# Three plain tiles instead of four ahead of the products of halves in four SwiGLU FFNs

## The chip, the cores and the metric

The kernel runs on one core of a Trainium2 chip. The metric is the device time of one execution in microseconds (us). TensorE multiplies, VectorE (DVE in the profile), ScalarE (ACT) and GpSimd (POOL) do elementwise work, SyncE (SP) issues the loads. Each engine works through its own queue in order and waits on semaphores.

## What is computed

A decoder trunk of two layers over 512 tokens and 16 prepended meta tokens, D = 1024, all in float32. Each layer is an FFN, a token mixer (gated linear attention in layer 0, windowed attention over shared keys and values in layer 1) and a second FFN; every part stands between two RMS norms and is added to the residual stream. The four FFNs are what the change is about:

```python
def rmsnorm(x, g):
    y = x * rsqrt(mean(x * x, axis=-1) + EPS)
    return y * g

def swiglu(x, w_in, w_out):              # D = 1024, D_FF = 2816
    gate, up = jnp.split(x @ w_in, 2, axis=-1)
    return (jax.nn.silu(gate) * up) @ w_out

h = h + 0.5 * rmsnorm(swiglu(rmsnorm(h, g[0]), w_ffn_in[layer, 0], w_ffn_out[layer, 0]), g[1])
```

## The kernel before

**Layout.** Tokens run along the free axis, features along the 128 partitions. `H` is the residual stream in eight tiles of 128 features (`KD`), `Y` a block's output. Layer 0 works on two groups of tokens, 272 and 256 (`L0`), layer 1 on 256 and 256 (`L1`) or on 512 at once (`L1W`). `D_FF` is cut into 22 tiles of 128 hidden features (`NFF`).

**Precision.** A float32 product is three matmuls on split operands: `hi` is a rounded copy, `lo` the difference; `hi*hi`, `lo*hi` and `hi*lo` add up in PSUM (`mm3s`, L344). Each split is a copy on ScalarE and a subtraction on VectorE: weights at L236 and L237 (`split_part`) or L255 and L256 (`split_pair`), hidden activations at L446 and L447.

**One FFN** (`ffn`, L754) goes through the hidden tiles in the chunks of `FF_CHUNKS`; after each chunk the hidden tiles so far are multiplied by their rows of `w_out` and added into `Y` (`out_steps`, L658).

- The first chunk, four tiles, is *plain*. `x_first` (L605) does two tiles on the first group of tokens and then on the second, while the block before still finishes; `x_units` (L580) does the two others. The operand `x` here isn't yet scaled by the norm's root: the result is, when it leaves PSUM (L767, L771), so these tiles can start before the root is known. Evacuation is two multiplications by the root, `silu`, a product and a split.
- The later chunks, three times six tiles, use *products of halves* (`class Strassen`, L867). The gate and up matrices of a tile, cut into two halves of D, are a 2 x 2 block matrix; the tokens in two halves make another. The 2 x 2 product takes seven products instead of eight. Each is 12 matmuls of 264 or 256 columns (`product`, L877). Their weights are sums of blocks, formed on VectorE by four additions (`add`, L261) and split into seven parts named 11, s1, s3, s2, 12, s4, 22 (`split_pair`, L246). A tile uses them in the order 11, s1, s2, 12, s3, then 11 of the next tile, s4, 22 (`head`, `body`, `tail`). Between them ScalarE copies bank `a` to `d` (L900) and banks to SBUF (L906, L908), and the products that follow overwrite these banks.

**The right-hand operand.** `right_factors` (L822) makes the operand of the halves while the plain tiles run: it waits for the roots of both groups (`x.rjob`), writes the normalized operand to `xs` with eight operations over all tokens (L847), and then, with differences of blocks (`less`, L843), splits seven operands called 11, t1, 22, t2, 21, t3 and t4 (`part`, L834 and L835). t3 and t4 wait until the plain tiles' matmuls are issued, since they use their space. `ffn` lets all of them be issued before the first product (L797).

**The roots.** At the end of the block before, `Residual.run` (L503) updates `H` group by group, builds the plain operand (`build`, L468 and L469) and sums the squares (L438, L441, L442). `factors` (L479) then makes the root and spreads it to 128 partitions: matmuls give the sums (`st`, L367), eleven or more small operations the root and a diagonal (L375 to L421), a matmul `r` spreads it (L429), and ScalarE copies it to `rt` (L491). `factors` uses GpSimd unless told otherwise; the very first FFN uses VectorE. Between FFN 2 (`l0f1`) or FFN 4 (`l1f1`) and its mixer the second group's root is made on GpSimd, `BEHIND` = 2.2 after the first step of its turn. FFN 3 (`l1f0`) uses the roots that the shared keys and values needed before it.

**What sets the order.** The order of TensorE is written out by the program. `Flow` (L70) keeps an estimated clock that each matmul advances, and side jobs (generators) say by `yield` how long until their next step; `flow.pump` issues what is due between matmuls, `flow.wait` issues jobs until one is finished. The other engines' instructions are ordered by the framework from this. Weights are loaded by SP into `RAWS` = 8 buffers of 512 columns; a split part occupies one of 32 buffers of the pool `hp`, as do z, hidden tiles and scratch. `set_ahead(n, slots)` (L219) limits how many weights are asked for and how many split parts may live at once: 4 in the plain tiles after `x_first`, 8 in the first output projection, `RING` = 10 among the products. `CHAINS` = 2 weight chains are made at once. The last chunk's rows of `w_out` come as `NLAST` units of another layout (`w_last`), read in one packed pass.

Of the kernel before, what the change touches and what calls it, by code (L numbers as in the profile page):

```python
# [13 lines left out]
ALU = mybir.AluOpType  # L14
# [3 lines left out]
D = 1024  # L18
KD = 8
# [1 line left out]
SEQ = 512  # L21
TOK = META + SEQ
NFF = 22
FF_CHUNKS = [(0, 4), (4, 10), (10, 16), (16, 22)]
LAST = 16
NLAST = NFF - LAST
HEADS = 4
RSQRT_MAGIC = float(0x5F3759DF)
# [2 lines left out]
L1W = [(16, 512)]  # L31
SLOTS = 32
RAWS = 8
RING = 10
STEP = 1.1
CHAINS = 2

# [11 lines left out]
NORM = 4.0  # L49
BUSY = 2.6  # L50
SHUT = 5.0
LOW = 1.0
LAG = 5
PERIOD = 3.2
# [79 lines left out]
def trunk_kernel(ctx: ExitStack, tc, a, out, last_out):  # L134
# [32 lines left out]
    def gain(layer, i, k):  # L167
        c = V_GAIN + layer * 48 + i * 8 + k
        return vec[:, c : c + 1]
# [49 lines left out]
    def set_ahead(n, slots=None):  # L219
        ahead[0], limit[0] = n, slots or n  # L220
        room[0].finish(flow)
        room[0] = Job(None)
# [226 lines left out]
    class Operand:  # L449


        def __init__(self, name, gv, groups, rt=None, parts=(1, 2)):
            self.parts = parts
            self.name, self.gv, self.groups, self.tiles = name, gv, groups, [None] * KD
            self.ready = set()
            self.rt = rt

            self.column = None
            self.more = LONGER
            self.rjob = [None] * len(groups)  # L460
            self.accs = [[] for _ in groups]

# [16 lines left out]
        def factors(self, gi, eng=pool):  # L479
            if self.column is not None:  # L480
                o, n = self.groups[gi]
                yield FACT + (ADDED if self.parts[gi] == 1 else 0)
                root(self.accs[gi], n, D, f"{self.name}_{o}", eng, *self.column[gi])
                yield CHAIN
                return
            if self.rt is None:
                self.rt = sm.tile([P, TOK], F32, tag="R", name=f"R_{self.name}", bufs=2)
            o, n = self.groups[gi]
            yield FACT + (ADDED if self.parts[gi] == 1 else 0)
            r = yield from rstd(self.accs[gi], n, D, False, f"{self.name}_{o}", eng, gi * BEHIND if eng is dve else self.more)  # L490
            act.activation(self.rt[:, o : o + n], r[:, :n], AF.Copy)  # L491

        def need(self, gi, k):
# [3 lines left out]
    class Residual:  # L497
# [5 lines left out]
        def run(self, gi, g, sums):  # L503
            o, n = g
            nxt = self.nxt
            if self.turned(gi):
                self.turn(g, sums)
                return
            yield 1.8 + (ADDED if self.parts[gi] == 1 else 0)
            r = yield from rstd(sums, n, D, self.half, f"post_{self.name}{gi}", dve)  # L510
            if nxt is None:
                yield from self.store(gi, g, r)
                return
            for k in range(KD):
                h, y = H[:, k, o : o + n], Y[:, k, o : o + n]
                t = r[:, 256 : 256 + n] if n <= 256 else ps(f"t_{self.name}{gi}{k}")[:, :n]
                dve.tensor_tensor(t, y, r[:, :n], op=ALU.mult)
                dve.tensor_tensor(h, t, h, op=ALU.add)
                nxt.build(gi, k)
                nxt.sumsq(gi, k)  # L520
                yield 1.0
            nxt.rjob[gi] = flow.spawn(nxt.factors(gi), gi * BEHIND)

        def store(self, gi, g, r):
            o, n = g
# [228 lines left out]
    def ffn(x, groups, finish, opening=False, tail=4):  # L754
        set_ahead(8 if opening else 16)

        def evac_to(hids):
            gss = {}

            def evac(i, g, p):  # L760
                o, n = g
                r = x.rt[:, o : o + n]
                if i % 2 == 0:
                    if i not in gss:
                        gss[i] = duo("gu")
                    gs = gss[i][0][:, o : o + n]
                    dve.tensor_tensor(gs, p[:, :n], r, op=ALU.mult)  # L767
                    act.activation(gs, gs, AF.Silu)
                else:
                    gs, us = (t[:, o : o + n] for t in gss[i - 1])  # L770
                    dve.tensor_tensor(us, p[:, :n], r, op=ALU.mult)  # L771
                    dve.tensor_tensor(us, gs, us, op=ALU.mult)
                    split(hids[i // 2], us, g)

            return evac

        jobs = []
        n2 = sum(n for _, n in groups) // 2
        halves = [(groups[0][0], n2), (groups[0][0] + n2, n2)]
        z, plain = {}, Job(None)  # L780

        def new_hid():
            hids.append(pair_tile(f"hid{x.name}_{lo + len(hids)}"))
            return hids[-1]

        for ci, (lo, hi) in enumerate(FF_CHUNKS):
            hids = []
            if ci == 0:
                jobs = x_first(x, 4, evac_to([new_hid() for _ in range(2)]), opening)
                set_ahead(16, 4)  # L790
                factors = flow.spawn(right_factors(x, halves, z, plain))
                for t in range(2, hi):
                    jobs += x_units(x, 2, groups, evac_to([new_hid()]))
                plain.finish(flow)
                set_ahead(16, 8)
            else:
                flow.wait(factors)  # L797
                set_ahead(16, RING)
                tiles = Strassen(z, halves)
                cur = tiles.head(new_hid())  # L800
                while cur:
                    last = len(hids) == hi - lo
                    if last:
                        fin = (finish, KD, True) if lo >= LAST else (None, 0, False)
                        proj = out_steps(hids, groups, x.groups, False, *fin, jobs)
                        end = used[0] + NLAST + tail
                    tiles.body(cur, (lambda: next(proj)) if last else (lambda: None))
                    nxt = None if last else tiles.head(new_hid())
                    jobs.append(tiles.tail(cur, last))
                    cur = nxt  # L810
            if ci == 0:
                out_proj(hids, groups, x.groups, True, jobs=jobs)
                continue
            if lo >= LAST:
                set_ahead(32)
                cap[0] = min(end, len(units))
            for _ in proj:
                pass
# [1 line left out]


    def right_factors(x, halves, z, plain):  # L822
        for job in x.rjob:
            yield job
        (o, n), _ = halves
        xs = [pair_tile(f"xs{x.name}_{k}", F32) for k in range(0, KD, 2)]
        blocks = [[t[:, :, i * n : (i + 1) * n] for t in xs] for i in range(2)]
        b11, b12, b21, b22 = blocks[0][:2], blocks[1][:2], blocks[0][2:], blocks[1][2:]

        def part(name, src, sign=1.0):  # L830
            z[name] = []
            for c, b in enumerate(src):
                w = pair_tile(f"z{x.name}_{name}{c}").rearrange("p a (k t) -> p a k t", k=2)[:, :, :, :n]
                act.activation(w[:, 0], b, AF.Copy, scale=sign)  # L834
                dve.scalar_tensor_tensor(  # L835
                    w[:, 1], b, sign, w[:, 0].bitcast(F32), op0=ALU.mult, op1=ALU.subtract
                )
                z[name].append(w)
                yield STEP

        def less(dst, p, q):
            for d, s, t in zip(dst, p, q):
                dve.tensor_tensor(d, s, t, op=ALU.subtract)  # L843
                yield STEP

        for k in (0, 1, 2, 3, 4, 5, 6, 7):
            dve.scalar_tensor_tensor(  # L847
                xs[k // 2][:, k % 2, : 2 * n], H[:, k, o : o + 2 * n], x.gv(k), x.rt[:, o : o + 2 * n],
                op0=ALU.mult, op1=ALU.mult,
            )  # L850
            yield 0.8
        yield from part("11", b11)
        yield from less(b11, b12, b11)
        yield from part("t1", b11, -1.0)
        yield from part("22", b22)
        yield from less(b12, b22, b12)
        yield from less(b22, b22, b11)
        yield from part("t2", b22, -1.0)
        yield from part("21", b21)
        yield from less(b21, b21, b22)  # L860
        yield plain
        yield from part("t3", b12)
        yield from part("t4", b21, -1.0)
# [618 lines left out]
    ffn(x, L0, fin, True)  # L1482
    x = nxt
    nxt, fin = into("l0f1", 0, 3, False, lambda k: gain(0, 4, k), L0)
    gla(x, fin)
    x = nxt
    nxt, fin = into("kv", 0, 5, True, lambda k: vec[:, V_KVN + k : V_KVN + k + 1], L0, (1, 1))
# [4 lines left out]
    with tc.tile_pool(name="kp", bufs=1) as kp:  # L1492
# [14 lines left out]
        ffn(x, L1W, fin)  # L1507
        x = nxt
        nxt, fin = into("l1f1", 1, 3, False, lambda k: gain(1, 4, k), L1, post=(2, 2))
        flow.wait(placed)  # L1510
        swa(x, kv, fin)
    ffn(nxt, L1W, Residual("out", 1, 5, True))
# [92 lines left out]
```

## Time and profile before

| | us |
|---|---|
| median of 3 runs | 1891.31 (1891.0 to 1892.04) |
| profiled execution, its time | 1890.36 |
| its span, first to last instruction | 1888.6 |
| VectorE busy | 1397.5 |
| ScalarE busy | 1017.7 |

The spans of the FFNs in the profile: the products of halves start at 84.8, 695.5, 1081.8 and 1595.9 us in FFN 1 to 4. How to read it: times in the profile count from the first instruction. PE is TensorE's matmuls, PEld its weight loads beside them. A row of the timeline gives start, length, engine, line, operation, output and inputs by name, shapes and a count, and in brackets the idle time of that engine just before and what ended it. A matmul's length holds the time that its result takes to come out, so the pace of a series is read from its starts. The same holds for VectorE: two operations that don't depend on each other start closer together than their length.

### The profile page before, as it was taken

The page shows a single profiled execution, that of the slowest core. Times are in us where ns is not written, and L with a number is a line of the kernel's source. Part 1 is how long each engine was busy: PE and PEld are TensorE (multiplying, and loading weights), DVE is VectorE, ACT ScalarE, POOL GpSimd, SP SyncE. Part 2 cuts the span into 40 slices and gives each one's busy share as a digit, 9 for nine tenths or more (in the row PEclk, how much of TensorE's full clock was granted, in tenths as well). Part 3 has the DMA queues.
Part 4 walks back from the last instruction along what each step waited for, and adds up shares of the span by engine and source line. Part 5 has one row for each costly group of instructions (what it writes and reads, how often), then busy time and mean ns, then how long its engine had stood idle before and what let it go on. Part 6 is the DMA issues. An engine that isn't in the chain of part 4 may idle for free.

```text
span 1888.6 us, 37662 instructions
## 1 busy us (share of the span) xinstructions
PE 1872.3 (99%) x14645; PEld 1791.3 (95%) x14645; DVE 1397.5 (74%) x2798; ACT 1017.7 (54%) x2273; POOL 196.0 (10%) x398
## 2 busy tenths in 40 slices
PE   8999999999999999999999999999999999999998
PEld 8999999999999999999999898989987898989898
DVE  7885858767564788585887886868766779868685
ACT  5653535653436566353574553535756855636364
POOL 2000000331311300000033000000320140000002
PEclk9999999999999999999999999999999999999999
DMA  4333232422113123233351223333421212333331
GB/s 165 97 98 103 90 107 96 137 68 66 48 59 121 46 90 96 90 101 101 100 175 46 72 86 112 93 110 101 135 74 51 69 46 73 97 106 103 104 113 57
DMA packets 102276, 174.74 MB, mean 93 GB/s; under 512 B 11856, under 2 KB 24016, under 8 KB 102096
## 3 DMA queue, kind: packets, MB, share of 16 engines
q1 hardware_dynamic: 101520, 171.67, 28.4%
q8 instruction: 115, 1.88, 0.4%
q10 hardware_dynamic: 576, 0.65, 0.1%
q14 instruction: 65, 0.53, 0.1%
HBM read 169.66 MB, written 2.10 MB: 91 GB/s over the span
## 4 chain that ended last, share of the span: by engine, by line
PE 87%; DVE 9%; ACT 2%; issue 2%; DMA 0%; POOL 0%; DVEq 0%; SPq 0%; ACTq 0%; POOLq 0%
PE y L172 30%; PE x L172 19%; PE a L172 18%; PE c L172 8%; PE d L172 4%; DVE raw L261 2%; ACT w_s L255 1%; PE o L172 1%; DVE w_s L256 1%; DVE w L256 1%; PE e L172 1%; DVE w L237 1%; PE po L172 1%; PE sa L172 1%; PE ps L172 0%
## 5 line engine op out<-in xcount | busy, mean ns | idle before, releaser
L256 DVE TENSOR_TENSOR w_s<-raw,w_s 128x512 fp32r<-128x512 f32 x288 | 193.8, 690 | 131.3 <-ACT w_s L255 128.9
L172 PE MATMUL y<-hidl0f,w 128*128 128x256 f32 (+1 forms) x2112 | 262.1, 285 | 1.1 <-DVE hidl0f L447 0.9
L172 PEld LDWEIGHTS y<-hidl0f,w 128*128 128x128 f32 x2112 | 259.1, 188 | 2.2 <-DVE hidl0f L447 1.5
L255 ACT ACTIVATE w_s<-raw 128x512 fp32r<-128x512 f32 x288 | 175.2, 628 | 152.3 <-DVE raw L261 139.1
L172 PE MATMUL y<-hidl1f,w 128*128 128x512 f32 (+1 forms) x1344 | 251.3, 346 | 0.3
L237 DVE TENSOR_TENSOR w<-raw,w 128x512 fp32r<-128x512 f32 x376 | 234.9, 654 | 21.9 <-ACT w L236 19.9
L172 PEld LDWEIGHTS y<-hidl1f,w 128*128 128x128 f32 x1344 | 212.7, 188 | 35.0 <-DVE hidl1f L933 1.5
L236 ACT ACTIVATE w<-raw 128x512 fp32r<-128x512 f32 x376 | 206.2, 586 | 39.3 <-PE y L172 29.3
L442 POOL TENSOR_TENSOR acc_post<-acc_post,sq_post 128x256 f32<-128x256 f32 (+1 forms) x77 | 62.9, 817 | 1458.2 <-ACT sq_post L441 1457.4
L261 DVE TENSOR_TENSOR raw<-raw,raw 128x512 f32<-128x512 f32 x288 | 198.0, 687 | 5.5
L256 DVE TENSOR_TENSOR w<-raw,w 128x512 fp32r<-128x512 f32 x216 | 148.4, 687 | 29.8 <-ACT w L255 29.0
L255 ACT ACTIVATE w<-raw 128x512 fp32r<-128x512 f32 x216 | 134.1, 621 | 41.1 <-PE y L172 40.7
L172 PE MATMUL x<-x_l0m,w 128*128 128x272 f32 (+1 forms) x1152 | 152.4, 289 | 0.0
L172 PEld LDWEIGHTS x<-x_l0m,w 128*128 128x128 f32 x1152 | 143.6, 189 | 1.5 <-issue 0.4
L697 DVE TENSOR_TENSOR Y<-y,Y 128x256 f32<-128x256 f32 (+2 forms) x175 | 81.9, 474 | 70.9 <-PE y L172 70.2
L172 PE MATMUL a<-zl0f_t,w_s 128*128 128x264 f32 x864 | 117.2, 285 | 0.0
L172 PE MATMUL a<-zl1f_t,w_s 128*128 128x256 f32 x864 | 114.3, 282 | 0.8 <-ACT c L908 0.5
L172 PEld LDWEIGHTS a<-zl0f_t,w_s 128*128 128x128 f32 x864 | 110.1, 188 | 0.3
L172 PEld LDWEIGHTS a<-zl1f_t,w_s 128*128 128x128 f32 x864 | 107.2, 188 | 2.5 <-ACT c L908 2.2
L172 PE MATMUL x<-x_l0f,w 128*128 128x256 f32 (+1 forms) x768 | 100.6, 291 | 6.2 <-ACT w L236 5.9
L172 PEld LDWEIGHTS x<-x_l0f,w 128*128 128x128 f32 x768 | 97.2, 193 | 7.6 <-ACT w L236 6.2
L172 PE MATMUL x<-x_l1f,w 128*128 128x256 f32 (+1 forms) x576 | 92.9, 321 | 0.0
(511 smaller groups left out, 3257.9 us busy)
## 6 DMA issues: line engine op xcount, KB each, us to landing
raw<-in_w_in SPq DMA_DIRECT2D x352, 256.0 KB, 2.9
raw<-in_w_out SPq DMA_DIRECT2D x96, 256.0 KB, 3.4
raw<-in_w_last SPq DMA_DIRECT2D x48, 256.0 KB, 3.0
raw<-in_gla_in SPq DMA_DIRECT2D x48, 256.0 KB, 3.0
raw<-in_w_out SPq DMA_DIRECT2D x64, 128.0 KB, 2.8
raw<-in_gla_out SPq DMA_DIRECT2D x16, 256.0 KB, 2.9
raw<-in_w_q SPq DMA_DIRECT2D x16, 256.0 KB, 3.8
raw<-in_swa_out SPq DMA_DIRECT2D x16, 256.0 KB, 3.0
```

The lines of the kernel that those rows point to most:

```text
L172: inst = pe.matmul(o, lhs, rhs, start=start, stop=stop, skip_group_check=onto)
L236: act.activation(w[:, 0, :m], raw[:, :m], AF.Copy)
L237: dve.tensor_tensor(w[:, 1, :m], raw[:, :m], w[:, 0, :m].bitcast(F32), op=ALU.subtract)
L255: act.activation(w[:, 0, :512], src, AF.Copy)
L256: dve.tensor_tensor(w[:, 1, :512], src, w[:, 0, :512].bitcast(F32), op=ALU.subtract)
L261: dve.tensor_tensor(dst, dst, src, op=ALU.add)
L442: pool.tensor_tensor(sums[0][:, :n], sums[0][:, :n], t[:, :n], op=ALU.add)
L697: dve.tensor_tensor(y, p[:, :n], y, op=ALU.add)
```

## The change

- `FF_CHUNKS` becomes three plain tiles and then chunks of 6, 6 and 7 tiles of products of halves. So one tile per FFN goes from the plain form to the products; the first output projection covers three tiles (384 columns of `w_out` per unit, not 512), the last one seven (`LAST` = 15, seven `w_last` units).
- `right_factors` writes the normalized operand group by group: after the first group's root eight operations on its tokens, after the second group's root eight on the others, not eight over all after both.
- For the operands of FFN 2 and FFN 4 (`late = dve`) the second group's root is made on VectorE and asked for without the delay `BEHIND`; `SPLIT` = 1.4 is the time allowed before the matmul that spreads it.
- `RING` is 16 less the tiles of the chunk: 10 for six tiles, as before, and 9 for seven.

```diff
-FF_CHUNKS = [(0, 4), (4, 10), (10, 16), (16, 22)]
-LAST = 16
+FF_CHUNKS = [(0, 3), (3, 9), (9, 15), (15, 22)]
+LAST = 15
...
-RING = 10
+RING = 16
...
+SPLIT = 1.4
...
             self.more = LONGER
+            self.late = pool
...
-            r = yield from rstd(self.accs[gi], n, D, False, f"{self.name}_{o}", eng, gi * BEHIND if eng is dve else self.more)
+            r = yield from rstd(self.accs[gi], n, D, False, f"{self.name}_{o}", eng, (SPLIT if self.late is dve else gi * BEHIND) if eng is dve else self.more)
...
-            nxt.rjob[gi] = flow.spawn(nxt.factors(gi), gi * BEHIND)
+            if gi and nxt.late is dve:
+                nxt.rjob[gi] = flow.spawn(nxt.factors(gi, dve))
+            else:
+                nxt.rjob[gi] = flow.spawn(nxt.factors(gi), gi * BEHIND)
...
-                set_ahead(16, RING)
+                set_ahead(16, RING - (hi - lo))
...
     def right_factors(x, halves, z, plain):
-        for job in x.rjob:
-            yield job
...
-        for k in (0, 1, 2, 3, 4, 5, 6, 7):
-            dve.scalar_tensor_tensor(
-                xs[k // 2][:, k % 2, : 2 * n], H[:, k, o : o + 2 * n], x.gv(k), x.rt[:, o : o + 2 * n],
-                op0=ALU.mult, op1=ALU.mult,
-            )
-            yield 0.8
+        for job, (og, ng) in zip(x.rjob, x.groups):
+            yield job
+            for k in range(KD):
+                dve.scalar_tensor_tensor(
+                    xs[k // 2][:, k % 2, og - o : og - o + ng], H[:, k, og : og + ng], x.gv(k), x.rt[:, og : og + ng],
+                    op0=ALU.mult, op1=ALU.mult,
+                )
+                yield 0.4
...
     nxt, fin = into("l0f1", 0, 3, False, lambda k: gain(0, 4, k), L0)
+    nxt.late = dve
...
         nxt, fin = into("l1f1", 1, 3, False, lambda k: gain(1, 4, k), L1, post=(2, 2))
+        nxt.late = dve
```

## The prediction

> **What bounds the kernel now.** I read the busy times and the chain of waits on the page first.
>
> ```profile
> PE 1872.3 (99%) x14645; PEld 1791.3 (95%) x14645; DVE 1397.5 (74%) x2798; ACT 1017.7 (54%) x2273; POOL 196.0 (10%) x398
> PE 87%; DVE 9%; ACT 2%; issue 2%; DMA 0%; POOL 0%; DVEq 0%; SPq 0%; ACTq 0%; POOLq 0%
> ```
>
> TensorE sets the time: less work for it is time won, if it is never kept waiting. DMA and GpSimd are no part of the chain. VectorE's 74% is a mean, so I took the busy time by stage. The first four windows run from the second group's roots (for the third FFN: from the end of its first two tiles) to the first product of halves of FFN 1 to 4; I call such a stretch a head. The fifth is six tiles of products. Columns: stretch, length, then busy time and instruction count of PE, weight loads, DVE, ACT, POOL, the clock, DMA share and GB/s.
>
> ```profile
> 40.55:84.75 44.20, 43.37 (x352) 42.72 (x351) 42.93 (x79) 27.29 (x61) 0.00 (x0) 1.00 0.29 91
> 655.15:695.50 40.35, 40.07 (x328) 39.81 (x327) 38.57 (x73) 25.19 (x57) 0.00 (x0) 1.00 0.24 73
> 1036.90:1081.83 44.93, 44.93 (x199) 36.53 (x198) 40.42 (x69) 24.08 (x46) 0.00 (x0) 1.00 0.21 67
> 1558.71:1595.86 37.15, 37.15 (x163) 30.02 (x161) 35.49 (x61) 22.14 (x42) 0.00 (x0) 1.00 0.22 71
> 84.75:148.20 63.45, 63.45 (x523) 63.45 (x522) 51.28 (x93) 37.41 (x80) 0.00 (x0) 1.00 0.33 105
> ```
>
> In the heads VectorE is busy 42.93 of 44.20, 38.57 of 40.35, 40.42 of 44.93 and 35.49 of 37.15 us; among the products only 51.28 of 63.45. So the heads are full on both engines, and the change shortens exactly these. DMA moves at a share of 0.33 at most, so loads are no limit.
>
> **What TensorE saves.** Timeline rows: start, length, line, tile, shape, count.
>
> ```profile
> 654.35 17.12 PE L172 MATMUL x<-x_l0f,w 128*128 128x272 f32 x138
> 675.79 19.75 PE L172 MATMUL y<-hidl0f,w 128*128 128x256 f32 x160 [0.28 <-DVE hidl0f L447]
> 695.50 1.62 PE L172 MATMUL a<-zl0f,w 128*128 128x264 f32 x12
> 696.97 1.63 PE L172 MATMUL c<-zl0f_t,w_s 128*128 128x264 f32 x12
> 1557.90 15.66 PE L172 MATMUL x<-x_l1f,w 128*128 128x512 f32 x66
> 1573.40 22.50 PE L172 MATMUL y<-hidl1f,w 128*128 128x512 f32 x96
> 1595.86 1.57 PE L172 MATMUL a<-zl1f,w 128*128 128x256 f32 x12
> 1597.27 1.59 PE L172 MATMUL c<-zl1f_t,w_s 128*128 128x256 f32 x12
> ```
>
> Layer 0: a plain tile is 96 matmuls, 272 and 256 columns in turn, at 17.12/138 = 0.123 us: 11.8 us. As products it is seven runs of 12 matmuls that start 1.47 us apart (695.50, 696.97): 10.3 us. Saved: 1.5 us. Layer 1: 48 matmuls of 512 columns; 66 of them take 1557.90 to 1573.40, 0.235 us each: 11.3 us; seven runs 1.41 us apart are 9.9 us. Saved: 1.4 us. The output projection has the same matmuls, only in other chunks. Four FFNs: 2 x 1.5 + 2 x 1.4 = **5.8 us** saved.
>
> [...]
>
> **What the shorter head costs.** The products begin earlier by the whole fourth plain tile and by its share of the first output projection: in layer 0 by 11.8 + 48 x 19.75/160 = 17.7 us, in layer 1 by 11.3 + 24 x 22.50/96 = 16.9 us. By then VectorE must have made the operands z. Its own relief, with the price of an operation taken as the distance of two starts:
>
> ```profile
> 1561.63 0.42 DVE L767 TENSOR_TENSOR gu<-x,R_l1f 128x256 f32<-128x256 f32 x1
> 1561.97 0.41 DVE L771 TENSOR_TENSOR gu<-x,R_l1f 128x256 f32<-128x256 f32 x1
> 1576.85 3.69 DVE L237 TENSOR_TENSOR w<-raw,w 128x512 fp32r<-128x512 f32 x6
> 40.55:84.75 44.20, 7.88 (x12) 1.00 0.29 91
> 655.15:695.50 40.35, 5.14 (x8) 1.00 0.24 73
> 1036.90:1081.83 44.93, 4.98 (x8) 1.00 0.21 67
> 1558.71:1595.86 37.15, 4.97 (x8) 1.00 0.22 71
> ```
>
> 256 columns cost 0.34 us; 512 cost (3.69-0.68)/5 = 0.60. The last four rows count the weight splits of L237 in each head.
> - Evacuating the fourth tile (L767, L771, L772, L447): layer 0 8 x 0.34 = 2.7 us, layer 1 4 x 0.60 = 2.4.
> - Weight splits: the fourth tile's four go, and the eight of the first projection narrow to 384 columns. No row has that width; between 0.34 and 0.60 I take 0.47. FFN 1: 12 x 0.60 - 8 x 0.47 = 3.4 us. In the others eight splits are done ahead of the roots; of the head's eight only four narrow ones stay: 8 x 0.60 - 4 x 0.47 = 2.9.
> - Operand by groups: the total is the same (eight operations of 528 columns become sixteen of half), but the first group's eight, some 8 x 0.34 = 2.7 us, can stand where VectorE waited for the second group's roots:
>
> ```profile
> 35.96 0.16 DVE L375 TENSOR_SCALAR av_l0f<-st_l0f 128x2 f32<-128x2 f32 x1 [3.04 <-PE st_l0f L172]
> 37.93 0.42 DVE L421 TENSOR_TENSOR dg_l0f<-ident,yv_l0f 128x256 f32<-128x256 f32 x1
> 40.55 0.42 DVE L767 TENSOR_TENSOR gu<-x,R_l0f 128x256 f32<-128x256 f32 x1 [2.20 <-ACT R_l0f L491]
> 655.15 0.42 DVE L767 TENSOR_TENSOR gu<-x,R_l0f 128x256 f32<-128x256 f32 x1 [4.85 <-ACT R_l0f L491]
> 1558.71 0.42 DVE L767 TENSOR_TENSOR gu<-x,R_l1f 128x256 f32<-128x256 f32 x1 [5.89 <-ACT R_l1f L491]
> ```
>
> The idle time was 2.2, 4.85 and 5.89 us in FFN 1, 2 and 4. In FFN 2 and 4 the roots move from GpSimd to VectorE: eleven operations, 35.96 to 38.35 in FFN 1, 2.4 us. Won: 2.2 in FFN 1, 4.85-2.4 = 2.5 in FFN 2, 5.89-2.4 = 3.5 in FFN 4. In FFN 3 both roots are there early and nothing is won.
>
> Relief: 2.7+3.4+2.2 = 8.3; 2.7+2.9+2.5 = 8.1; 2.4+2.9 = 5.3; 2.4+2.9+3.5 = 8.8 us, each against 17.7 or 16.9. The rest must come from what was early before. The operand t3 is the last z that a first tile needs soon: its second split (L835) beside the product that reads it, FFN by FFN:
>
> ```profile
> 79.99 0.70 DVE L835 SCALAR_TENSOR_TENSOR zl0f_t<-xsl0f,zl0f_t 128x528 fp32r<-128x528 f32 x1
> 90.62 1.64 PE L172 MATMUL a<-zl0f_t,w_s 128*128 128x264 f32 x12
> 692.78 1.32 DVE L835 SCALAR_TENSOR_TENSOR zl0f_t<-xsl0f,zl0f_t 128x528 fp32r<-128x528 f32 x2
> 701.36 1.62 PE L172 MATMUL a<-zl0f_t,w_s 128*128 128x264 f32 x12
> 1076.37 0.68 DVE L835 SCALAR_TENSOR_TENSOR zl1f_t<-xsl1f,zl1f_t 128x512 fp32r<-128x512 f32 x1
> 1087.49 1.58 PE L172 MATMUL a<-zl1f_t,w_s 128*128 128x256 f32 x12
> 1596.14 1.28 DVE L835 SCALAR_TENSOR_TENSOR zl1f_t<-xsl1f,zl1f_t 128x512 fp32r<-128x512 f32 x2
> 1602.21 1.70 PE L172 MATMUL a<-zl1f_t,w_s 128*128 128x256 f32 x12 [0.53 <-ACT c L908]
> ```
>
> It was early by 9.9, 7.3, 10.4 and, counted to 1601.5 (four runs of 1.41 after 1595.86), 4.1 us; FFN 4 already lost 0.7 there. Short: 17.7-8.3-9.9 = -0.5, so 0; 17.7-8.1-7.3 = 2.3; 16.9-5.3-10.4 = 1.2; 16.9-8.8-4.1 = 4.0. Sum 7.5 us, less the old 0.7: **6.8 us** of new waiting.
>
> Bounds of the shortage. If VectorE's idle time inside the heads (1.3, 1.8, 4.5, 1.7 us from the windows) also fills, 0, 0.5, 0 and 2.3 are left: 2.8, less 0.7. The upper end is the slower rival below.
>
> An added wait: the second group's sums (st) now stand some 2 us earlier on TensorE in FFN 2 and 4, and in FFN 4 they need ScalarE's last square:
>
> ```profile
> 1548.16 0.40 ACT L438 ACTIVATE acc_l1f<-H 128x256 f32<-128x256 f32 x1
> 1549.82 0.95 PE L172 MATMUL st_l1f<-ones,acc_l1f 128*128 128x1 f32 x8
> ```
>
> From 1549.82 back to about 1547.6 is before 1548.56, so x matmuls queued behind st can wait up to 1.0 us. VectorE's small root operations wait for st in turn and hold the weight splits behind them. I cost both at nothing of their own: TensorE's loss there gives VectorE the same time before the products. RING - (hi - lo) is 10 for six tiles as before and 9 for seven: one weight part less in stock, which costs nothing while VectorE has 12 us to spare per six tiles, and up to one run (1.4 us) per FFN without. The seven last units are two more loads and splits, taken from the other projections. No load is moved past another but the weights in their new order, and the roots leave GpSimd's queue, which does nothing else in the heads.
>
> **The sum.** 6.8 - 5.8 = +1.0 us on the profiled execution of 1890.36 us (span 1888.6): 1891.4. The median shown, 1891.31, is 0.95 above that execution: **1892.3 us**. A measurement can tell about 0.2%, 3.8 us: same is 1887.5 to 1895.1.
>
> **Rivals.**
> - *The cover holds* (0.30, faster). VectorE catches up in its idle time, and operations that the first tile doesn't need yet fall behind z. For it: 9.3 us of idle time in the four heads. Against it: much of that is waiting for ScalarE and TensorE within a chain. It gives 1890.4-5.8+0.95 = 1885.5; with the lower shortage above, 1887.6.
> - *ScalarE's queue turns lateness into a stall one product sooner and more* (0.31, slower). The third product overwrites bank a, so the copy d<-a (L900) must be through, 2.9 us before t3 is read. That copy stands on ScalarE among splits that wait for VectorE:
>
> ```profile
> 1597.99 0.37 ACT L900 ACTIVATE d<-a 128x256 f32<-128x256 f32 x1
> 1600.46 1.15 ACT L255 ACTIVATE w_s<-raw 128x512 fp32r<-128x512 f32 x2 [2.10 <-DVE raw L261]
> ```
>
>   There L900 came just ahead of a 2.10 us wait for L261, and the next copies stood behind it, which made the 0.7 us. If the backlog stands ahead of L900, each FFN loses 2.9 us more: 4 x 2.9 - 0.5 = 11.1, 1903.4 us. It decides once VectorE is over 3 us late at the first product.
> - *Narrow matmuls dearer* (0.01, still within 0.2%): if layer 1's products ran at the plain tiles' 0.123 us of layer 0 instead of 0.118, 84 x 0.005 x 2 = 0.9 us go: 1893.2. [...]
>
> **Chances.** Forecast 0.38, with the narrow matmuls 0.39: within 0.2%. Faster 0.30, slower 0.31. The range reaches from the full saving to the slower rival, 1885.5 to 1903.
>
> **What would show it.** Right: TensorE busy falls by about 6 us; VectorE has no idle time left before the products; first-tile products wait for z or for L900, most in FFN 4, least in FFN 1. Wrong: first tiles run at 1.41 and 1.47 us without gaps (the saving comes whole), or the wait reaches 3 us and more in every FFN; also wrong if gaps appear inside later tiles or in the seven-tile chunk.

## The result, and the profile after

| | before | after |
|---|---|---|
| median, us | 1891.47 (5 runs) | 1919.36 (1918.96 to 1921.27, 5 runs) |
| ratio | 1 | 1.0144, 95% interval 1.0132 to 1.0156 |
| span of the profiled execution, us | 1888.6 | 1917.6 |
| mean granted TensorE clock | 1.000 | 0.993 |

The kernel became 1.4% slower, 28 us; forecast was no change, and at worst 1903. First the page of the changed kernel, the same two lines as before.

```profile
PE 1880.9 (98%) x14741; PEld 1801.9 (94%) x14741; DVE 1420.4 (74%) x2884; ACT 1031.9 (54%) x2303; POOL 194.2 (10%) x374
PE 75%; DVE 15%; ACT 6%; issue 2%; POOL 1%; DMA 0%; DVEq 0%; SPq 0%; ACTq 0%; POOLq 0%
```

In the chain TensorE has gone from 87% to 75%, VectorE from 9% to 15%, ScalarE from 2% to 6%: TensorE now waits for both, in turn. DMA is still no part of it. TensorE's busy time rose instead of falling, above all because some 24 us of the span ran at half clock (last section). The 96 matmuls more are 48 for the products and 48 for the output projection of layer 1, where 48 of 512 columns became 96 of 256.

Where the time came in, from the start of each stage's first projection in the two traces: FFN 1 (from the start of the span) +3.6 us, the mixer of layer 0 +2.4, FFN 2 +8.9, the projections of keys and values 0, FFN 3 +4.9, the mixer of layer 1 +2.2, FFN 4 +7.6; together 29.6 of a span that grew by 29.0. Most of each FFN's loss lies before the sixth product of the first tile. Timeline of TensorE around the first product in FFN 1, changed kernel:

```profile
67.15 0.29 PE L173 MATMUL d<-zeros 128*128 128x264 f32 x1
67.28 1.63 PE L173 MATMUL a<-zl0f,w 128*128 128x264 f32 x12
68.75 1.62 PE L173 MATMUL c<-zl0f_t,w_s 128*128 128x264 f32 x12
72.81 3.01 PE L173 MATMUL a<-zl0f_t,w_s 128*128 128x264 f32 x12 [2.44 <-ACT d L905]
75.62 1.84 PE L173 MATMUL d<-zl0f,w 128*128 128x264 f32 x12
77.30 1.61 PE L173 MATMUL a<-zl0f_t,w_s 128*128 128x264 f32 x12
78.75 1.64 PE L173 MATMUL a<-zl0f,w 128*128 128x264 f32 x12
```

The third product waits 2.44 us, and not for its operand but for the copy d<-a on ScalarE (L905; L900 before). Then twelve matmuls take 2.81 us (72.81 to 75.62) instead of 1.47. The same places in all FFNs, in us after the first product, from the traces:

| | FFN 1 | FFN 2 | FFN 3 | FFN 4 |
|---|---|---|---|---|
| t3 ready, before | -4.1 | -1.4 | -4.8 | 1.6 |
| t3 ready, by my sum | 5.3 | 8.2 | 6.8 | 9.7 |
| t3 ready, after | 8.8 | 7.8 | 9.9 | 9.2 |
| fifth product (reads t3) starts, after | 10.0 | 8.9 | 11.0 | 10.3 |
| sixth product starts, before | 7.4 | 7.3 | 7.1 | 7.9 |
| sixth product starts, after | 11.5 | 10.5 | 12.5 | 11.8 |
| lost in the first tile | 4.1 | 3.2 | 5.4 | 3.9 |

That is 16.6 us. The second place is the head of FFN 2 and FFN 4, ahead of the products. Timelines of the changed kernel, TensorE and then VectorE:

```profile
660.21 1.22 PE L173 MATMUL r_l0f<-dg_l0f,ones 128*128 128x256 f32 x2 [4.31 <-DVE dg_l0f L422]
```

```profile
654.55 1.02 DVE L238 TENSOR_TENSOR w<-raw,w 128x384 fp32r<-128x384 f32 x2
655.48 0.16 DVE L376 TENSOR_SCALAR av_l0f<-st_l0f 128x2 f32<-128x2 f32 x1
655.55 0.50 DVE L852 SCALAR_TENSOR_TENSOR xsl0f<-H,vec,R_l0f 128x272 f32<-128x272 f32 x1
655.96 0.17 DVE L379 TENSOR_SCALAR yv_l0f<-av_l0f 128x2 int32<-128x2 int32 x1
656.03 0.50 DVE L852 SCALAR_TENSOR_TENSOR xsl0f<-H,vec,R_l0f 128x272 f32<-128x272 f32 x1
...
659.74 0.42 DVE L422 TENSOR_TENSOR dg_l0f<-ident,yv_l0f 128x256 f32<-128x256 f32 x1
```

The matmul that spreads the second group's root (r_l0f) stands in TensorE's queue and holds the x matmuls behind it for 4.31 us. The root is late because its first operation stood behind weight splits (L238), and because each further one takes a turn with an operation of the operand (L852): 655.48 to 660.16 is 4.7 us for a chain that took 2.4 alone. In FFN 4 TensorE waits twice, for the last square on ScalarE and for the root:

```profile
1570.55 0.94 PE L173 MATMUL st_l1f<-ones,acc_l1f 128*128 128x1 f32 x6 [1.41 <-ACT acc_l1f L439]
1578.98 0.70 PE L173 MATMUL r_l1f<-dg_l1f,ones 128*128 128x256 f32 x2 [1.04 <-DVE dg_l1f L422]
```

The three waits are 6.8 us, and two windows of half clock behind them (659.76 and 1571.12) cost some 3 more, an estimate: half of TensorE's busy time in them.

### The profile page after: what moved, and what is told of

It reads as the page before. It is cut to its first block, busy times and chain, and to the rows that moved or that the text cites. A ratio compares the mean times of both kernels' runs of the same rounds, so it can differ in the third digit from the quotient of the medians.

```text
span 1917.6 us, 37962 instructions
## 1 busy us (share of the span) xinstructions
PE 1880.9 (98%) x14741; PEld 1801.9 (94%) x14741; DVE 1420.4 (74%) x2884; ACT 1031.9 (54%) x2303; POOL 194.2 (10%) x374
## 4 chain that ended last, share of the span: by engine, by line
PE 75%; DVE 15%; ACT 6%; issue 2%; POOL 1%; DMA 0%; DVEq 0%; SPq 0%; ACTq 0%; POOLq 0%
PE y L173 29%; PE x L173 15%; PE a L173 14%; PE c L173 6%; DVE raw L262 4%; PE d L173 3%; DVE w_s L257 3%; ACT w_s L256 3%; DVE w L257 2%; PE o L173 1%; DVE w L238 1%; PE e L173 1%; PE po L173 1%; ACT w L237 1%; PE sa L173 1%
## 5 line engine op out<-in xcount | busy, mean ns | idle before, releaser
L257 DVE TENSOR_TENSOR w_s<-raw,w_s 128x512 fp32r<-128x512 f32 x304 | 204.6, 691 | 129.6 <-ACT w_s L256 127.8
L256 ACT ACTIVATE w_s<-raw 128x512 fp32r<-128x512 f32 x304 | 185.2, 629 | 175.6 <-DVE raw L262 162.4
L238 DVE TENSOR_TENSOR w<-raw,w 128x512 fp32r<-128x512 f32 (+1 forms) x368 | 224.8, 644 | 22.1 <-ACT w L237 20.0
L237 ACT ACTIVATE w<-raw 128x512 fp32r<-128x512 f32 (+1 forms) x368 | 198.7, 578 | 41.5 <-PE y L173 30.6
L262 DVE TENSOR_TENSOR raw<-raw,raw 128x512 f32<-128x512 f32 x304 | 209.2, 688 | 5.8
L257 DVE TENSOR_TENSOR w<-raw,w 128x512 fp32r<-128x512 f32 x228 | 156.8, 688 | 28.2 <-ACT w L256 27.2
L256 ACT ACTIVATE w<-raw 128x512 fp32r<-128x512 f32 x228 | 141.5, 621 | 41.5 <-PE y L173 41.2
L905 ACT ACTIVATE d<-a 128x264 f32<-128x264 f32 (+1 forms) x76 | 28.2, 371 | 112.6 <-PE a L173 112.3
L173 PE MATMUL x<-x_l0f,w 128*128 128x272 f32 (+1 forms) x576 | 77.7, 295 | 7.0 <-ACT w L237 5.7
L173 PEld LDWEIGHTS x<-x_l0f,w 128*128 128x128 f32 x576 | 74.3, 195 | 8.5 <-ACT w L237 5.9
```

The source lines that it names most:

```text
L173: inst = pe.matmul(o, lhs, rhs, start=start, stop=stop, skip_group_check=onto)
L237: act.activation(w[:, 0, :m], raw[:, :m], AF.Copy)
L238: dve.tensor_tensor(w[:, 1, :m], raw[:, :m], w[:, 0, :m].bitcast(F32), op=ALU.subtract)
L256: act.activation(w[:, 0, :512], src, AF.Copy)
L257: dve.tensor_tensor(w[:, 1, :512], src, w[:, 0, :512].bitcast(F32), op=ALU.subtract)
L262: dve.tensor_tensor(dst, dst, src, op=ALU.add)
```

## Which part costs what

Theory A: the shorter head leaves VectorE too little time, whatever the other two parts do. Theory B: the roots on VectorE make the loss. The three parts were tried one by one and in pairs. Their edits against the changed kernel:

```diff
# three tiles -> four tiles
-FF_CHUNKS = [(0, 3), (3, 9), (9, 15), (15, 22)]
-LAST = 15
+FF_CHUNKS = [(0, 4), (4, 10), (10, 16), (16, 22)]
+LAST = 16
# roots on VectorE -> on GpSimd (two places)
-    nxt.late = dve
# operand by groups -> whole width after both roots
-        for job, (og, ng) in zip(x.rjob, x.groups):
-            yield job
-            for k in range(KD): ...
+        for job in x.rjob: yield job
+        for k in (0, 1, 2, 3, 4, 5, 6, 7):
+            dve.scalar_tensor_tensor(xs[k // 2][:, k % 2, : 2 * n], H[:, k, o : o + 2 * n], ...)
```

Three tiles alone:


> Three plain tiles and the new chunks alone; the normalized operand after both roots and the second roots on GpSimd, as before. Theory A (the shorter head starves the first tile of products: VectorE and ScalarE make z and the weight parts too late): the four first tiles lose about 16 us together, as in the changed kernel, and perhaps 2 to 6 more since nothing is made early; less the saved 5.8, 1901 to 1908. Theory B (the root chain moved to VectorE is the cause): the saving comes whole, 1885 to 1887.


Three tiles and groups:


> The change without its third part: the second roots of FFN 2 and FFN 4 stay on GpSimd. If TensorE's waits for the root on VectorE (4.3 us at 660, 1.5 and 1.0 us at 1570 to 1579, and the halved clock after two of them) come from that part, 9 to 11 us go away: about 1909. If the first tiles alone are the cause, 1917 to 1921.


Three tiles and roots on VectorE:


> The change without its second part: all of the normalized operand after both roots, the roots on VectorE. If the operations of the first group, which stand between the steps of the root chain, are what makes that chain slow (4.7 us from its first to its last step, not 2.4), the wait at the root falls from 4.3 to about 2 us in FFN 2 and goes away in FFN 4, but z comes some 2 us later in FFN 1 and 4: 1912 to 1919. If they don't matter, 1919 to 1925.


Groups and roots, four tiles:


> The change with four plain tiles again: operand by groups and the second roots on VectorE alone. Theory A: the first tiles have no waits; what is left is the root's wait: 1891.5 plus 5 to 11, 1897 to 1902. Theory B is the same here. If the root's wait comes only with the shorter head, 1889 to 1892.


Groups alone:


> Four plain tiles and the operand by groups, both roots as before (the second on GpSimd). If the roots on VectorE are what cost the four-tile kernel its 9.5 us (its trace: 4.4 us of TensorE waiting before r_l0f, 2.8 before r_l1f, 1.5 before st_l1f, three clock windows at 0.5), those waits are gone and the groups alone gain what the first FFN gained there, 1.7 us, and the 0.7 us of the last FFN: 1888 to 1890 us. If the groups themselves cost, by sixteen dearer operations in the head: 1893 us or more.


Roots alone:


> Four plain tiles, second roots on VectorE, operand in whole-width operations after both roots. If the root operations lose their time behind weight splits in VectorE's queue, the waits before r_l0f and r_l1f are there also without the groups: 1896 to 1901 us. If they lose it by taking turns with the operand's operations, which here all stand behind them, the chain is 2.4 us as it was for the first FFN: 1890 to 1893 us.

| plain tiles | operand by groups | roots on VectorE | median, us | ratio to before (95%) |
|---|---|---|---|---|
| 4 | yes | no (e5) | 1889.73 | 0.9988 (0.9979 to 0.9996) |
| 4 | no | yes (e6) | 1896.53 | 1.0025 (1.0015 to 1.0034) |
| 4 | yes | yes (e4) | 1900.27 | 1.0047 (1.0032 to 1.0062) |
| 3 | no | no (e1) | 1924.05 | 1.0168 (1.0151 to 1.0185) |
| 3 | yes | no (e2) | 1918.47 | 1.0141 (1.0126 to 1.0157) |
| 3 | no | yes (e3) | 1915.83 | 1.0135 (1.0120 to 1.0150) |
| 3 | yes | yes (the change) | 1919.36 | 1.0144 (1.0132 to 1.0156) |

The three tiles alone cost 1.68%, 32 us, more than the whole change; I had put that run at 1901 to 1908 at most, so theory A held and its size was far off. Theory B as the whole cause is out, since e1 has no root on VectorE. The five other runs fell inside one of the ranges given for them.

What the two other parts are worth depends on what stands beside them. The operand by groups gains while the roots stay on GpSimd: 0.12% with four tiles, with the interval below 1; with three it points the same way, 0.27%, the intervals overlapping a little. Beside roots on VectorE it costs 0.22% with four tiles (e6 to e4, the intervals just touching) and nothing clear with three (e3 to the change). The roots on VectorE cost with four tiles (0.25% without groups, 0.59% with them, e4 against e5). With three tiles they cost nothing beside the groups (e2) and gain 0.33% without them (e1 to e3, intervals apart). The likely reason: a wait in the head gives VectorE time that the first tile then doesn't have to give. **The version with groups alone and four tiles beats both kernels, by little.**

The wait before the root's matmul in FFN 2 tells why. One row of TensorE's timeline each: e5, e6, e4.

```profile
653.48 0.70 PE L173 MATMUL r_l0f<-dg_l0f,ones 128*128 128x256 f32 x2 [0.40 <-POOL dg_l0f L422]
```

```profile
652.52 0.70 PE L173 MATMUL r_l0f<-dg_l0f,ones 128*128 128x256 f32 x2 [2.26 <-DVE dg_l0f L422]
```

```profile
652.65 1.22 PE L173 MATMUL r_l0f<-dg_l0f,ones 128*128 128x256 f32 x2 [4.25 <-DVE dg_l0f L422]
```

On GpSimd the root is 0.40 us late; behind VectorE's weight splits 2.26; taking turns with the operand as well, 4.25. So both halves of what e6 was to tell apart are true, about equally. GpSimd is the slower engine for these operations (in e5 they take 5.0 us, 648.37 to 653.42, against VectorE's 2.4), but its queue was empty.

## Two gates in a row

With three tiles, what holds the first tile? Theory Q: ScalarE's queue, in which the copy d<-a stands behind splits (my slower rival). Theory V: VectorE is simply not done with t3. Theory H: the half clock after the pause. Two runs, made from the changed kernel, put twelve extra matmuls, the first product over again, between second and third product of a chunk's first tile: e7 into d, so that the copy isn't needed; e8 into a bank that nobody reads, with the copy kept.

```diff
             self.product(t.a, t, "11", "11", True)
-            act.activation(self.d, t.a, AF.Copy)                # e7 only
+            if len(self.tiles) > 1:
+                act.activation(self.d, t.a, AF.Copy)
...
+            if len(self.tiles) == 1:
+                for k in range(4):
+                    ...
+                    mm(self.d, wh, xh, k == 0, False)           # e8: self.c[1]
+                    mm(self.d, wl, xh, False, False)
+                    mm(self.d, wh, xl, False, k == 3)
             self.product(t.a, t, "s2", "t2", False)
```

> The changed kernel, but in the first tile of halves of each FFN the copy d<-a on ScalarE is replaced by computing the same product once more, into d (12 matmuls, 1.43 to 1.47 us). If the third product waited for ScalarE's queue, it now starts when t2 is there, 4.4 to 5.1 us after the first instead of 4.5 to 6.4, without a halved clock, and the sixth when t3 is there plus one run, 10.2 to 11.3 instead of 10.5 to 12.5: 3 to 5 us less than the changed kernel, 1914 to 1917 us. If the operands alone set the pace: no gain, 1918 to 1920 us.

> The changed kernel with the same 12 extra matmuls in the first tile of each FFN at the same place, but into an unused bank, and the copy d<-a left where it was. The third product still waits for the copy, as late as before, but TensorE's pause ahead of it is 1.45 us shorter. If a long pause halves the clock and this cost time, the windows at 0.5 in the first, third and fourth FFN go and the kernel gains up to 1.7 us in each where the halved run was not itself hidden by waiting for t3: 1915 to 1918 us. If the halved runs were hidden: 1919 us and the windows gone all the same.

Measured 1935.53 us (ratio 1.0231, 1.0217 to 1.0245) and 1929.68 (1.0201, 1.0187 to 1.0215). Both lie above the ranges expected, and these totals mislead: an FFN has three chunks of products, and the eight sets of matmuls in second and third chunks stood in no wait, 8 x 1.45 = 11.6 us. The first tiles can be read nevertheless. Timeline of TensorE in e7, FFN 1, from the third product on:

```profile
71.54 1.63 PE L173 MATMUL a<-zl0f_t,w_s 128*128 128x264 f32 x12
73.00 1.62 PE L173 MATMUL d<-zl0f,w 128*128 128x264 f32 x12
77.02 2.64 PE L173 MATMUL a<-zl0f_t,w_s 128*128 128x264 f32 x12 [2.40 <-ACT c L921]
```

Without the copy the third product starts 4.4 us after the first, not 5.5. Nothing is won: the fifth starts 9.9 us after it, as in the changed kernel (10.0), and in the other FFNs at 9.0, 11.0 and 10.6 (8.9, 11.0, 10.3). The wait has only moved from the third product to the fifth. There it is for t3 (ready at 8.7) and then, some 1.1 us longer, for ScalarE's copies of the second and third product (L921 is the latter), which stand behind the splits of t3 and t4 and two weight splits (L256). ScalarE in e7:

```profile
75.28 1.13 ACT L256 ACTIVATE w_s<-raw 128x512 fp32r<-128x512 f32 x2
76.32 0.37 ACT L912 ACTIVATE c<-c 128x264 f32<-128x264 f32 x1
76.59 0.38 ACT L921 ACTIVATE c<-a 128x264 f32<-128x264 f32 x1
```

So opening Q at the third product alone gives nothing.

In e8 half clock left the first tiles of FFN 1 and 4 but not that of FFN 3: the fourth product is 1.62 and 1.59 us long in the first two, 2.77 in the last (from 1095.70). So theory H got a clean run, with the spare matmuls in the first chunk of products alone:

> The changed kernel with the 12 spare matmuls in the first tile of the first chunk of products alone (the run before had them in each of the three chunks of an FFN, 8 sets of 1.45 us outside any wait, 11.6 us). If the halved clock in the first tile costs nothing, because the fifth product waits for VectorE's chain anyway: 1918 to 1920 us, with no window at 0.5 in the first tiles of FFN 1 and 4. If it costs: 1915 us or less.

Measured 1918.19 us (ratio 1.0142, 1.0127 to 1.0158). No window of half clock is left in a first tile (in FFN 1 the third product takes 1.57 us to the start of the fourth, not 2.81), and the time is that of the changed kernel. Its TensorE in FFN 1:

```profile
72.84 1.74 PE L173 MATMUL a<-zl0f_t,w_s 128*128 128x264 f32 x12 [0.95 <-ACT d L906]
74.41 1.62 PE L173 MATMUL d<-zl0f,w 128*128 128x264 f32 x12
77.18 1.73 PE L173 MATMUL a<-zl0f_t,w_s 128*128 128x264 f32 x12 [1.15 <-ACT c L921]
```

At full clock TensorE reaches the fifth product sooner and waits 1.15 us for it; it starts at 77.18 against 77.30. The sixth products start 11.4, 10.5, 12.4 and 11.8 us after the first, in the changed kernel 11.5, 10.5, 12.5 and 11.8. H costs nothing there: the product at half clock lay inside the next wait.

Then VectorE. e9 is e2 (three tiles, groups, roots on GpSimd) without the eight differences of blocks (L846), so its products use other operands than they should. e10 is e2 with nothing left out, the differences on GpSimd.

```diff
-                dve.tensor_tensor(d, s, t, op=ALU.subtract)
+                pool.tensor_tensor(d, s, t, op=ALU.subtract)    # e10; the line is left out in e9
```

> Three plain tiles and groups, second roots on GpSimd, with the eight differences of blocks of xs (L846, some 5.0 us of VectorE in each head) left out, so that the products use wrong operands. If VectorE's work between the operand and t3 is what makes the first tiles late (in the kernel that it is made from their sixth products start 4.1, 4.0, 5.4 and 7.6 us late, 21 us in all), 5 us go in each: 0, 0, 0.4 and 2.6 are left, and 1918.5 becomes about 1900 us. If the narrow matmuls, the queue of ScalarE or the halved clock made the loss by themselves, it stays within 5 us of 1918.5.

> The same three tiles, nothing left out: the eight differences are made by GpSimd, which is idle in the heads. VectorE is relieved of the same 5 us, but a difference of 512 columns takes some 1.6 us on GpSimd (it takes 0.82 for 256), and t2 and t3 stand behind two and four of them in a row. If VectorE's load decides: 1900 to 1906 us. If the chain of the differences decides, because its own length grows by some 5 us: 1915 us or more.

e9 gave 1913.75 us (1.0118, 1.0103 to 1.0133), only 4.7 less than e2: theory V alone fell too. t3 was ready 6.1, 6.1, 7.4 and 7.4 us after the first product, 2.5 to 3.5 earlier than in e2, and the sixth product started 11.2, 11.7, 12.8 and 13.9 after it all the same. ScalarE and then TensorE of e9 in FFN 1:

```profile
69.17 0.64 ACT L837 ACTIVATE zl0f<-xsl0f 128x528 fp32r<-128x528 f32 x1
69.70 2.24 ACT L837 ACTIVATE zl0f_t<-xsl0f 128x528 fp32r<-128x528 f32 x4
71.83 0.38 ACT L904 ACTIVATE d<-a 128x264 f32<-128x264 f32 x1
```

```profile
68.57 1.62 PE L173 MATMUL c<-zl0f_t,w_s 128*128 128x264 f32 x12
72.26 2.19 PE L173 MATMUL a<-zl0f_t,w_s 128*128 128x264 f32 x12 [2.08 <-ACT d L904]
```

The first product ended near 68.7, but its copy stood behind five more splits of the operand, those of t3 and t4 among them, which nobody needed yet: 71.83. This is the rival's mechanism in the open. The program writes the whole operand into the queues before the first product, so ScalarE has it all ahead of the copy.

Here H isn't free, though. TensorE's rows go on:

```profile
74.25 2.73 PE L173 MATMUL d<-zl0f,w 128*128 128x264 f32 x12
76.81 1.64 PE L173 MATMUL a<-zl0f_t,w_s 128*128 128x264 f32 x12
```

The fifth product starts without a wait, t3 having been ready for 3.7 us, but 4.55 us after the third, where two products take 2.94 at full clock (e12 below); the fourth alone takes 2.56 (74.25 to 76.81), not 1.48, so I put it down to half clock. In the other FFNs it is 4.6, 4.5 and 5.3. So in e9 the waits for the copy (2.08, 2.62, 3.90 and 3.89 us) cost 12.5 us, and the half clock that follows these pauses some 7 more, an estimate: the four distances less two products each at full clock.

e10 gave 1941.45 us (1.0265, 1.0247 to 1.0282), worse than any and far inside "1915 us or more". A difference took 1.6 us on GpSimd, as expected, but ScalarE's splits waited for it with the copy behind them:

```profile
79.03 0.64 ACT L837 ACTIVATE zl0f_t<-xsl0f 128x528 fp32r<-128x528 f32 x1 [0.42 <-POOL xsl0f L846]
81.35 0.64 ACT L837 ACTIVATE zl0f_t<-xsl0f 128x528 fp32r<-128x528 f32 x1 [1.68 <-POOL xsl0f L846]
81.90 0.37 ACT L905 ACTIVATE d<-a 128x264 f32<-128x264 f32 x1
```

In FFN 1 the third product waited 5.59 us. The last run opens both gates: e9, with the copy replaced as in e7, in the first tile of each FFN alone.

> The kernel without the eight differences (1913.8 us; its operands were ready early, t2 1.6 to 3.8 and t3 6.1 to 7.4 us after the first product, and yet the third product started 5.2 to 6.9 us after it, behind the copy d<-a on ScalarE), now also with that copy replaced by computing the product once more, in the first tile of each FFN alone. If VectorE's work and ScalarE's queue are two gates in a row, of which either alone holds the first tile back, this opens both: the sixth product starts some 8.9 us after the first instead of 11.2 to 13.9, 2.3 to 5.0 us less in each FFN, and the time is 1898 to 1902 us, 5.8 of it for the 48 extra matmuls. If a third thing holds the tile (the copies of the second and third product, or the weights): 1908 us or more.

Measured 1902.67 us (1.0052, 1.0035 to 1.0069), 0.7 above its range: 11 us less than e9, although it does 48 matmuls more. TensorE in FFN 1:

```profile
66.94 1.63 PE L173 MATMUL a<-zl0f,w 128*128 128x264 f32 x12
68.41 1.62 PE L173 MATMUL c<-zl0f_t,w_s 128*128 128x264 f32 x12
69.87 1.64 PE L173 MATMUL d<-zl0f,w 128*128 128x264 f32 x12
71.34 1.62 PE L173 MATMUL a<-zl0f_t,w_s 128*128 128x264 f32 x12
72.80 1.64 PE L173 MATMUL d<-zl0f,w 128*128 128x264 f32 x12
74.28 1.68 PE L173 MATMUL a<-zl0f_t,w_s 128*128 128x264 f32 x12
75.79 1.62 PE L173 MATMUL a<-zl0f,w 128*128 128x264 f32 x12
```

The sixth product starts 8.85 us after the first, the extra 1.47 included; in the other FFNs 8.8, 9.2 and 9.2. No half clock falls in a first tile: in FFN 1 the products start 1.46 to 1.51 us apart. Opening VectorE's gate alone won 4.7 us, opening both won 15.8, and the extra matmuls (48 x 0.121 = 5.8) hide part of that. Opening ScalarE's gate at the third product alone won nothing (e7's first tiles; e7 has the second roots on VectorE, e9 and e12 on GpSimd, which is 0.9 us between e2 and the changed kernel). Two gates in a row it is, and the half clock that followed the pause at the first in e9 goes with it. Even so, with 5 us of VectorE's work per FFN left out, three tiles don't get ahead of four: 1902.67 - 5.8 = 1896.9, where the kernel before took 1890.3 to 1893.7 beside it. Of the 13 us that the span of e12 has more than that of before, 5.8 are the extra matmuls and 4.4 the two mixers.

## Why the prediction was wrong, step by step

**TensorE saves 5.8 us: nearly right.** Summed over the distances of starts, before against e12, the 192 plain matmuls fewer in layer 0 took 23.0 us and the 96 in layer 1 22.2; 168 more matmuls of products in each cost 20.5 and 20.0 us at 0.122 and 0.119. Saved: 4.7. "The same matmuls" in the output projection was wrong for layer 1, at next to no cost: 48 at 0.233 became 96 at 0.119. The narrow matmuls were as cheap as the rows of before said (1.47/12 = 0.123 and 1.41/12 = 0.118 us); that rival is out.

**VectorE's relief, 8.3, 8.1, 5.3 and 8.8 us: the step that failed.** FFN 3 shows it purest, since none of its roots was moved. Windows from the operand's first operation to the second split of t3; columns: stretch, length, VectorE busy and count, clock, DMA share and GB/s. Before: the operand (L847), the splits (L256) and the sums (L261) of the products' own weights:

```profile
1035.63:1077.05 41.42, 5.75 (x8) 1.00 0.18 58
1035.63:1077.05 41.42, 3.43 (x5) 1.00 0.18 58
1035.63:1077.05 41.42, 2.14 (x4) 1.00 0.18 58
```

After, the same three (L852, L257, L262):

```profile
1049.20:1090.00 40.80, 6.77 (x16) 0.96 0.16 52
1049.20:1090.00 40.80, 5.43 (x8) 0.96 0.16 52
1049.20:1090.00 40.80, 4.13 (x6) 0.96 0.16 52
```

I had forecast a stretch 5.3 us shorter; it shrank by 0.6. The evacuation and the first projection's splits did fall, by 2.7 and 3.0 us of busy time. But the first tile's own weights are due when the products start, and with the products earlier they went ahead of t3 in VectorE's queue: six operations more (the fourth sum of before starts at 1076.97, behind t3's last split), some 3.6 us at 0.60 from start to start. I had counted the weight splits that leave the head and not those that the products bring into it. The operand by groups cost 1.0 more, and idle time grew by 0.9. In FFN 1 five such operations came in too, in FFN 2 and 4 four and three.

VectorE's idle time, which my lower bound of the shortage let fill, is 5.0 us in this stretch. One wait makes most of it, and the splits of the operand stand behind it in VectorE's queue, though the operand was written by 1060.3:

```profile
1058.65 1.67 DVE L852 SCALAR_TENSOR_TENSOR xsl1f<-H,vec,R_kv 128x256 f32<-128x256 f32 x4
1063.54 0.69 DVE L776 TENSOR_TENSOR gu<-x,R_kv 128x512 f32<-128x512 f32 x1 [3.22 <-PE x L173]
```

So the order of the queue may have its share in t3's lateness beside the amount of work. That isn't shown: no run here tried another order.

In FFN 2 and 4 the forecast for t3 (8.2 and 9.7) is right by luck: the root's wait had held TensorE up and so given VectorE the time. With the roots on GpSimd (e2) t3 came at 8.7 and 10.9.

**t3 sets the end: right, but not alone.** The fifth product was the gate, as e7 and e11 show. It started 1.1 to 1.3 us after t3 was ready, 4.5 us over four FFNs that my sum didn't have: ScalarE's copies of the products stand behind the operand's last splits and two weight splits. The whole shortage at the fifth product was 17 us (4.1, 3.0, 5.3, 4.6 later than four runs in a row), against 7.5 forecast: 3 us and more in every FFN, as my sign of being wrong had it.

**The slower rival: the right mechanism, under-priced.** It had the copy behind the splits, and that VectorE's lateness decides; it took 2.9 us per FFN and 1903.4 in all. It treated the copy as an addition to VectorE's lateness, where the two lie partly over each other, and took the lateness too small.

**Roots on VectorE, a gain of 2.5 and 3.5 us, and their waits at nothing: the second step that failed.** I priced eleven operations back to back and counted the engine's idle time as theirs. In that time TensorE had x matmuls to do, which now stood behind the root's matmul: 4.31 us in FFN 2, 1.04 in FFN 4. The added wait for st is there too, 1.41 us. I had put these waits at nothing of their own, since VectorE gains the time. In part it does: against e2 the sixth product comes 0.9 us sooner in FFN 2 and 2.9 in FFN 4. But by the spans of the profiled runs FFN 2 as a whole takes 3.3 us more than in e2, and only FFN 4 takes 1.0 less. Without the groups they gain about what I forecast (e1 to e3: 2.9 and 3.6 us less, half clock included); it is beside the groups, as in the change, that the step fails.

**What the miss is made of.** An estimate from the figures above, in us: first tiles 16.6, waits in the heads 6.8 and half clock there some 3, mixers 4.6, five smaller waits of TensorE (at 6.59, 16.48, 338.22, 959.54 and 988.93) 2.8, together 33.8; less 4.7 saved it is 29, the growth of the span. The forecast had 6.8 for the first tiles, nothing for the rest, and 5.8 saved.

**RING 9 and the seven-tile chunk cost nothing: nearly.** A wait of 0.4 us came in before the last chunk's end in FFN 1 and 2, none inside the six-tile chunks.

**Not foreseen:** the mixers. Every kernel with three tiles waits 1.7 us before r_go in layer 0 (GpSimd's dg_go), none with four does; the new order of weights and side work reaches that far. Which edit in that order makes it late was not tried. Layer 1's 2.2 us are half clock: the window of 6.83 us in the last section costs 3.1, and a wait of 0.7 before is gone. In e11, which has no such window, the same stretch is 0.8 us shorter than before.

## What to carry to other kernels

When a stage is made to start earlier, count what it needs from the other engines at that earlier time, its own weights too, and not only what the shortened stage no longer does. A stall's releaser names the gate that opens last, not the only one: here removing either of two gates won little (nothing in e7's first tiles, 4.7 us in e9), removing both won 16 us (e12). With four tiles the small dependent operations did best on a queue that was empty when they were due, even on a slower engine (5.0 us of work on GpSimd against 2.4 on VectorE, and yet 1889.73 us in e5 against 1900.27 in e4); with three, what they lost in the head came back in part at the first tile (0.9 and 2.9 us in FFN 2 and 4). A part's worth in one version of a kernel is not its worth in another.

## What the hardware showed

TensorE's clock was halved behind some of its pauses, and one of these was far shorter than the stretch that followed: 0.88 us before 6.83. Windows of the changed kernel: stretch, length, busy time of PE, weight loads, DVE, ACT, POOL, clock, DMA share and GB/s.

```profile
72.67:76.08 3.41, 3.27 (x15) 3.27 (x16) 3.41 (x7) 1.97 (x5) 0.00 (x0) 0.50 0.00 0
659.76:663.17 3.41, 2.96 (x11) 2.78 (x12) 1.68 (x5) 0.96 (x3) 0.00 (x0) 0.50 0.01 4
1530.16:1536.99 6.83, 6.68 (x35) 5.18 (x36) 3.27 (x13) 1.20 (x3) 0.00 (x0) 0.50 0.00 0
```

The clock was 0.50 for 3.41 us, or twice that, after pauses of 2.44 us (72.81) and 4.31 (660.21), and not after one of 1.44 us at 693.97. Yet one of 1.41 us at 1570.55 was followed by half clock (1571.12), and the third row follows one of 0.88 us at 1530.31, which the kernel before has at 1511.41 without any effect (clock 1.00 from there to 1520.00): here the length of the pause alone doesn't decide. The trace's six windows (72.67, 659.76, 1086.43, 1530.16, 1571.12, 1612.08) begin 587.09, 426.67, 443.73, 40.96 and 40.96 us apart, which is 172, 125, 130, 12 and 12 times 3.4133 us (40.96/12). Whether it matters where in this grid a pause falls, no run here shows. The price depended on what followed: nothing ahead of another wait (the fifth product starts at 77.30 us, and at 77.18 in e11 without half clock), some 7 us in e9, while in FFN 1 of e7 the sixth product came 2.44 us after the fifth (77.02, 79.46) instead of 1.47.
